# Input norm of an encoder trunk: two token tiles transposed through diag(1/rms), the gain moved to the split, and a written order on four engines

## The chip, the cores and the metric

The kernel runs on one core of a Trainium2 chip. The core has TensorE (PE, matrix products), VectorE (DVE), ScalarE (ACT), GpSimd (POOL) and SyncE (SP), which here only issues DMAs. Each engine works through its own queue in order. The metric is the device time of one execution in microseconds.

## The reference, cut to what matters

One layer of an encoder on 512 tokens of 1024 channels, in float32: a token mixer (HGRN2 and mLSTM heads behind one input projection), cross-attention to 256 memory tokens, an MLP with squared ReLU, and a final norm. The change touches only the first norm and the first use of what it gives:

```
def rmsnorm(x, g):
    y = x32 * lax.rsqrt(jnp.mean(x32 * x32, axis=-1, keepdims=True) + NORM_EPS)
    return (y * g.astype(jnp.float32)).astype(x.dtype)

proj = rmsnorm(x, norm_mix) @ w_in + b_in
```

`1/rms` belongs to a token, the gain `g` (`norm_mix`) to a channel. The columns of the projection that come first are 1536 to 2047, the value `h_i` of HGRN2 (512 columns), needed with the tokens on the partitions.

## The kernel before, in words

**Numbers.** A big product keeps float32 precision by splitting both operands into a rounded high half and a low half (`split_out`, lines 227 to 229: ACT copies the high half, DVE subtracts it from the source for the low half) and adding three products, high by high, high by low and low by high (`mm3`, lines 231 to 234). A split of a tile from PSUM reads it twice, once on each engine.

**The weights** come as a stream of blocks of 128 x 1024 floats (512 KB). `load(i)` (line 203) issues the DMA of block i on SP into one of three `st` buffers; `split(i)` (line 210) makes its halves `wh` and `wl`, three buffers each. `weights(key)` asks for the block, splits it and the two next, and loads the one after them.

**The first stage, lines 135 to 325.** x comes in four tiles of 128 tokens by 1024 channels, two in each of two `as` buffers (`xin`, `xtile`). Tile by tile: ACT squares the tile and sums along the row (line 297); DVE makes the mean square (line 172) and POOL takes its power of -1/2 (line 174, `rstd_of`); DVE multiplies each half of the tile with 1/rms, a number for each partition, and the gain, which stands in two PSUM banks of 512 columns that are the same on all partitions (`gmix`, line 144: products of a column of ones with the row of gains; line 302). PE turns the half over, four transposes of 128 x 128 against the identity (line 305), and `split_out` writes the halves into `xT`, where the channels are on the partitions. For channel block k, `xT[k // 4]` holds 512 columns of high half and 512 of low half, one for each token.

The projection of the 512 value columns (`proj_t`, line 258) takes four weight blocks q = 0 to 3, of two channel blocks each. A *part* (t, q) is the six products of token tile t with weight block q, summed in PSUM bank `acc[t]`. It runs q = 0, 1, 2 over all four t, then q = 3, where each t ends and is evacuated by DVE with a bias added (line 324). The bias is loaded in line 318 into a `T2` buffer of 516 columns, of which there are five. PSUM has four banks `mm` and four banks `sm`. The next stage is the product for the gates (lines 511 and 512), and behind it the other columns of the projection.

`small_setup` (line 146) loads the small vectors `vc` and the level masks, and makes some small constants on DVE and ACT. The identity is part of `cs`, 392 columns of constants loaded by ACT's queue (line 139).

**The order of the work.** The kernel is written with a tile framework: a planner puts the instructions of each engine in an order, by priority (`tc.high_priority`) and by when its plan finds their inputs ready, and inserts the waits. Only the MLP at the end has PE's order fixed as written (`tc.manual_schedule`, line 991).

Of the kernel before, what the change touches and what calls it, by code (L numbers as in the profile page):

```python
# [18 lines left out]
P = 128  # L19
S = 512  # L20
D = 1024
# [18 lines left out]
C_ID, C_MF, C_MB, C_SEL, NC1 = 0, 128, 256, 384, 392  # L40
# [39 lines left out]
def trunk(ctx: ExitStack, tc: tile.TileContext, x, mem, wpk, vec, cst, lmask, rmask, rows, out):  # L80
    nc = tc.nc
    big = ctx.enter_context(tc.tile_pool(name="big", bufs=1))
    sb = ctx.enter_context(tc.tile_pool(name="sb", bufs=1))
    psm = ctx.enter_context(tc.tile_pool(name="psm", bufs=4, space=PSUM))
    pss = ctx.enter_context(tc.tile_pool(name="pss", bufs=4, space=PSUM))
    v, sc, gp, pe = nc.vector, nc.scalar, nc.gpsimd, nc.tensor
    cnt = [0]

    def nm(s):
        cnt[0] += 1  # L90
        return f"{s}_{cnt[0]}"
# [28 lines left out]
    cs = sb.tile([P, NC1], F32, name="cs")  # L120
# [13 lines left out]
    def load_x(t):  # L134
        nc.sync.dma_start(out=xtile[t], in_=x[t * P:t * P + P, :])

    load_x(0)
    nc.scalar.dma_start(out=grow1[0:1, :], in_=rows[0:1, :])
    nc.scalar.dma_start(out=cs, in_=cst[:, 0:NC1])
    one1 = misc[0:1, 63:64]  # L140
    gp.memset(one1, 1.0)
    gmix = [mmb(), mmb()]
    for g in range(2):
        pe.matmul(gmix[g], lhsT=one1.to_broadcast([1, P]), rhs=grow1[0:1, g * 512:g * 512 + 512], start=True, stop=True)

    def small_setup():
        lmf = A4()
        nc.sync.dma_start(out=vc, in_=vec)
        nc.sync.dma_start(out=lmf[:, 0:len(LEVELS) * P], in_=lmask)
        for j in range(2):  # L150
            a = lmf[64 * j:64 * j + 64, 64 * j:NLV * P]
# [10 lines left out]
        v.tensor_copy(selr[0:64, :], cs[0:64, C_SEL:C_SEL + 8])  # L162
        v.tensor_copy(selr[64:128, :], cs[0:64, C_SEL:C_SEL + 8])
        v.tensor_scalar(out=negb, in0=vc[:, V_FF:V_FF + 8], scalar1=-1.0, scalar2=None, op0=ALU.mult)
# [5 lines left out]
    def rstd_of(ss, w, n):  # L170
        ms = tiny(w)
        v.tensor_scalar(out=ms, in0=ss, scalar1=1.0 / n, scalar2=EPS, op0=ALU.mult, op1=ALU.add)  # L172
        r = tiny(w)
        gp.tensor_tensor(out=r, in0=ms, in1=nh.to_broadcast([P, w]), op=ALU.pow)  # L174
        return r, ms
# [51 lines left out]
    def split_out(dst_hi, dst_lo, src):  # L227
        sc.activation(dst_hi, src, AF.Copy)  # L228
        v.tensor_tensor(out=dst_lo, in0=src, in1=dst_hi.bitcast(F32), op=ALU.subtract)  # L229

    def mm3(ps, ah, al, bh, bl, first, last):
        pe.matmul(ps, lhsT=ah, rhs=bh, start=first, stop=False)  # L232
        pe.matmul(ps, lhsT=ah, rhs=bl, start=False, stop=False)  # L233
        pe.matmul(ps, lhsT=al, rhs=bh, start=False, stop=last)  # L234
# [23 lines left out]
    def proj_t(mat, k0, c0, xs, ntile=4, pre=None, late=False):  # L258

        acc = [mmb() for _ in range(ntile)]  # L260

        def part(t, q, w):
            for k in range(2):
                kk = 2 * q + k
                xh, xl = xs[kk][0][:, t * P:t * P + P], xs[kk][1][:, t * P:t * P + P]
                z = slice(k * 512, k * 512 + 512)
                mm3(acc[t], xh, xl, w[0][:, z], w[1][:, z], kk == 0, kk == 7)

        for q in range(2 if late else 3):
            w = weights(("t", mat, k0 + 2 * q, c0))  # L270
            for t in range(ntile):
                part(t, q, w)
                if t % 2 == 1:
                    tick()
        if pre is not None:
            pre()
        tail = [(q, weights(("t", mat, k0 + 2 * q, c0))) for q in range(2 if late else 3, 4)]
        for t in range(ntile):
            for q, w in tail:
                part(t, q, w)  # L280
            yield t, acc[t]
            if t % 2 == 1:
                tick()


    xT = XT()
    load(0)
    load_x(1)
    load_x(2)
    load(1)  # L290
    load_x(3)

    junk = G4()
    for t in range(4):
        xt = xtile[t]
        ss = tiny(1)
        sc.activation(junk, xt, AF.Square, accum_out=ss)
        r, _ = rstd_of(ss, 1, D)
        with tc.high_priority():
            for g in range(2):  # L300
                xg = xt[:, g * 512:g * 512 + 512]
                v.scalar_tensor_tensor(out=xg, in0=xg, scalar=r, in1=gmix[g], op0=ALU.mult, op1=ALU.mult)
                ps = smb()
                for k in range(4):
                    pe.transpose(ps[:, k * P:k * P + P], xg[:, k * P:k * P + P], ident)
                p3 = ps[:, :].rearrange("p (k t) -> p k t", t=P)
                split_out(ap(xT[g], t * P, [1024, 4], [1, P]), ap(xT[g], 512 + t * P, [1024, 4], [1, P]), p3)
        if t < 2:
            split(t)
    small_setup()  # L310
    xs = xk(xT)


    vh = []

    def bias_row(i):
        b = T2()
        nc.sync.dma_start(out=b[:, 0:512], in_=rows[1 + i // 2:2 + i // 2, (i % 2) * 512:(i % 2) * 512 + 512].to_broadcast([P, 512]))
# [298 lines left out]
    def mv_proj():  # L617
        b = bias_row(1)
        for t, ps in proj_t("in", 0, 3584, xs):
            d = VV()  # L620
            gp.memset(ap(d, P, [129, 4], [1, 1]), 1.0)
            v.tensor_tensor(out=ap(d, 0, [129, 4], [1, P]), in0=ps[:, :].rearrange("p (h e) -> p h e", e=P),
                            in1=b[:, 0:512].rearrange("p (h e) -> p h e", e=P), op=ALU.add)
            mv.append(d)

    mq = {}
# [127 lines left out]
    for t in range(2):  # L754
        a = mt[t]
# [31 lines left out]
    for c in range(2):  # L787
        for t, ps in proj_t("kv", 0, 1024 + 512 * c, ms, 2):
            d = A4(F32R)
# [101 lines left out]
    for h in range(4):  # L891
        qd[h] = []
        for ps in proj_d("xq", 256 * h, x2):
            d = YT1()
# [97 lines left out]
    for f in range(4):  # L992
# [72 lines left out]
        while n < len(JOBS):  # L1065
            p, g = JOBS[n]
# [8 lines left out]
            w = ahead(n)  # L1075
# [95 lines left out]
```

## Time and profile before

| what | value |
|---|---|
| median of 3 runs (lowest to highest) | 861.6 us (861.53 to 861.63) |
| the profiled execution: its own time | 861.55 us |
| its span, first to last instruction | 859.8 us |
| PE busy in the span | 839.1 us (98%) |
| DVE, ACT, POOL busy | 566.8, 422.8, 67.4 us |
| granted PE clock, mean | 0.996 |
| time from HBM | 110.76 MB, 131 GB/s |

A row of a timeline has the start and the duration in us, the engine, the line, the operation, the tile written and the tiles read, their shape and how many instructions were merged; in brackets stands the idle time before it and what ended that. "L305" is line 305 of the kernel. Durations of PE overlap, as its instructions are pipelined, so the distance between starts says how fast it works. "PEld" is the load of the stationary operand, "SPq" and "ACTq" a DMA being issued on that engine's queue.

### The profile page before, as it was taken

The numbers are of one execution on the slowest core, as the hardware profiler recorded it, in microseconds if no ns is written. First come the engines' busy times: TensorE is split into PE (matmuls) and PEld (weight loads), VectorE is DVE, ScalarE is ACT, GpSimd is POOL, SyncE is SP. The second block draws the span as 40 slices with busy tenths as digits, with TensorE's granted clock in tenths as the row PEclk, the third lists the DMA queues.
The fourth block names the chain that finished last, engine by engine and source line by source line (L and its number), as shares of the span: only waits on it lengthen the run. The fifth ranks groups of instructions, "written<-read, shape, count | busy, mean of one in ns | idle before, by whom it ended". The sixth has DMA issues, their size and how long they took to land.

```text
span 859.8 us, 11677 instructions
## 1 busy us (share of the span) xinstructions
PE 839.1 (98%) x4438; PEld 692.3 (81%) x4438; DVE 566.8 (66%) x996; ACT 422.8 (49%) x773; POOL 67.4 (8%) x114
## 2 busy tenths in 40 slices
PE   7999999999999999999999999999999999999994
PEld 5888788788887987887888887888888888888883
DVE  5558874699437977654555446676667656756675
ACT  5336354445558576454443346453454344434544
POOL 1000000100100000100001200003101210220001
PEclk9999999999999999999999999999999999999998
DMA  6332224022252332542213852248935992697322
GB/s 265 126 117 78 70 77 139 31 74 88 80 141 74 99 125 98 177 117 98 74 50 117 201 147 82 95 132 234 277 112 142 276 243 98 177 290 193 123 50 98
DMA packets 32682, 113.62 MB, mean 132 GB/s; under 512 B 3761, under 2 KB 3889, under 8 KB 32626
## 3 DMA queue, kind: packets, MB, share of 16 engines
q1 hardware_dynamic: 23120, 78.84, 26.4%
q0 software_dynamic: 9216, 33.56, 17.7%
q8 instruction: 35, 0.57, 0.3%
q10 hardware_dynamic: 290, 0.47, 0.2%
q14 instruction: 21, 0.17, 0.1%
HBM read 110.76 MB, written 2.10 MB: 131 GB/s over the span
## 4 chain that ended last, share of the span: by engine, by line
PE 72%; issue 21%; DVE 3%; POOL 1%; DMA 1%; ACT 1%; POOLq 0%; ACTq 0%; DVEq 0%
PE mm L233 15%; PE mm L232 15%; PE mm L234 15%; PE sm L1045 5%; PE sm L1046 5%; PE sm L1047 5%; PE sm L682 2%; PE sm L667 2%; PE sm L380 1%; POOL tiny L174 1%; PE mm L1046 1%; PE mm L1045 1%; PE mm L1047 1%; PE sm L450 1%; DVE wl L229 1%
## 5 line engine op out<-in xcount | busy, mean ns | idle before, releaser
L228 ACT ACTIVATE wh<-st 128x1024 fp32r<-128x1024 f32 x133 | 141.0, 1060 | 222.7 <-PE mm L233 118.0
L229 DVE TENSOR_TENSOR wl<-st,wh 128x1024 fp32r<-128x1024 f32 x133 | 162.8, 1224 | 116.0 <-ACT wh L228 110.9
L232 PE MATMUL mm<-xT,wh 128*128 128x512 f32 x544 | 215.6, 397 | 0.0
L233 PE MATMUL mm<-xT,wh 128*128 128x512 f32 x544 | 213.2, 392 | 0.3 <-DVE xT L824 0.3
L234 PE MATMUL mm<-xT,wl 128*128 128x512 f32 x544 | 212.5, 391 | 0.0
L233 PEld LDWEIGHTS mm<-xT,wh 128*128 128x128 f32 x544 | 102.2, 188 | 22.9 <-DVE xT L824 2.0
L232 PEld LDWEIGHTS mm<-xT,wh 128*128 128x128 f32 x544 | 102.2, 188 | 22.2 <-issue 0.7
L234 PEld LDWEIGHTS mm<-xT,wl 128*128 128x128 f32 x544 | 102.1, 188 | 21.4 <-issue 0.2
L939 POOL DMA_DIRECT2D as<-in_wpk x48 | 36.5, 771 | 312.5 <-DVE wl L229 186.7
L1003 DVE SCALAR_TENSOR_TENSOR t<-mm,rg 128x512 f32<-128x512 f32 x32 | 22.1, 691 | 55.1 <-PE mm L234 55.0
L234 PE MATMUL mm<-wh,yT 128*128 128x512 f32 x128 | 50.6, 395 | 0.0
L232 PE MATMUL mm<-wh,yT 128*128 128x512 f32 x128 | 50.4, 394 | 0.0
L233 PE MATMUL mm<-wl,yT 128*128 128x512 f32 x128 | 50.0, 391 | 0.0
L1045 PE MATMUL sm<-wh,yT 128*128 128x512 f32 x128 | 49.8, 389 | 0.0
L1046 PE MATMUL sm<-wl,yT 128*128 128x512 f32 x128 | 49.8, 389 | 0.0
L1047 PE MATMUL sm<-wh,yT 128*128 128x512 f32 x128 | 49.8, 389 | 0.0
L228 ACT ACTIVATE wh<-as 128x1024 fp32r<-128x1024 f32 x24 | 25.5, 1062 | 33.3 <-PE sm L1047 23.7
L229 DVE TENSOR_TENSOR wl<-as,wh 128x1024 fp32r<-128x1024 f32 x24 | 29.4, 1225 | 13.9 <-ACT wh L228 13.9
L174 POOL TENSOR_TENSOR tiny<-tiny,misc 128x1 f32<-128x1 f32 (+1 forms) x18 | 14.2, 788 | 299.0 <-DVE tiny L172 299.0
L978 DVE TENSOR_TENSOR vv<-vv,sm 128x512 f32<-128x512 f32 x48 | 31.0, 680 | 1.2 <-PE sm L1047 1.2
L228 ACT ACTIVATE yT<-t 128x512 fp32r<-128x512 f32 x32 | 19.8, 629 | 17.0 <-DVE t L1020 16.5
L1045 PEld LDWEIGHTS sm<-wh,yT 128*128 128x128 f32 x128 | 24.0, 188 | 5.0
(273 smaller groups left out, 1503.4 us busy)
## 6 DMA issues: line engine op xcount, KB each, us to landing
st<-in_wpk SPq DMA_DIRECT2D x133, 512.0 KB, 3.4
as<-in_wpk POOLq DMA_DIRECT2D x48, 512.0 KB, 6.6
gate<-in_wpk POOLq DMA_DIRECT2D x16, 512.0 KB, 7.0
as<-in_x SPq DMA_DIRECT2D x4, 512.0 KB, 6.5
vv<-in_x SPq DMA_DIRECT2D x8, 256.0 KB, 3.6
out<-vv SPq DMA_DIRECT2D x7, 256.0 KB, 2.3
a<-in_mem SPq DMA_DIRECT2D x2, 512.0 KB, 5.8
t<-in_rows SPq DMA_DIRECT2D x2, 256.0 KB, 6.1
```

The source lines that it names most:

```text
L174: gp.tensor_tensor(out=r, in0=ms, in1=nh.to_broadcast([P, w]), op=ALU.pow)
L228: sc.activation(dst_hi, src, AF.Copy)
L229: v.tensor_tensor(out=dst_lo, in0=src, in1=dst_hi.bitcast(F32), op=ALU.subtract)
L232: pe.matmul(ps, lhsT=ah, rhs=bh, start=first, stop=False)
L233: pe.matmul(ps, lhsT=ah, rhs=bl, start=False, stop=False)
L234: pe.matmul(ps, lhsT=al, rhs=bh, start=False, stop=last)
L939: gp.dma_start(out=dst, in_=wpk[idx], **kw)
L978: v.tensor_tensor(out=z, in0=z, in1=ps, op=ALU.add if sign > 0 else ALU.subtract)
L1003: v.scalar_tensor_tensor(out=y, in0=ps, scalar=0.0, in1=rrow[:, 0:512], op0=ALU.max, op1=ALU.mult)
L1045: pe.matmul(ps, lhsT=ah, rhs=bh, start=new, stop=False, **fl)
L1046: pe.matmul(ps, lhsT=ah, rhs=bl, start=False, stop=False, **fl)
L1047: pe.matmul(ps, lhsT=al, rhs=bh, start=False, stop=end and k == 1, **fl)
```

## The change

1. **Gain.** The two banks of broadcast gains go. Eight products of one column each put the gain on the partitions, channel block by channel block, in `gk` (128 x 8), which ACT copies out of PSUM. The gain is multiplied in when the turned tile is split (`x_split`): ACT's copy takes it as its scale, and DVE's instruction becomes a `scalar_tensor_tensor`.
2. **Tiles 0 and 1** are not scaled. DVE makes diag(1/rms) from the identity (`x_diag`), and the turn is an ordinary float32 product of the tile with that matrix (`x_turn`), which scales as it transposes. **Tiles 2 and 3** are scaled by DVE with 1/rms alone (`x_scale`) and transposed as before.
3. **Halves.** A split takes 256 columns: one channel block of two token tiles (0 and 1, then 2 and 3). A PSUM bank holds two channel blocks of a token half, so that four banks hold a half.
4. **Order.** From the first square to part (1, 2) the order on PE, DVE, ACT and POOL is the order in which the code is written (`tc.manual_schedule`). The other parts follow in `proj_vh`.
5. **Loads.** ACT's queue loads the identity alone; the other constants follow on SP inside `small_setup`. Block 1 is loaded ahead of tile 2, and block 2 behind tile 3.
6. **Setup and bias** go behind the split of the second half. The masks are loaded into the buffer of tiles 0 and 1, the bias into that of tile 2.

```diff
-    nc.scalar.dma_start(out=cs, in_=cst[:, 0:NC1])
+    nc.scalar.dma_start(out=ident, in_=cst[:, C_ID:C_ID + P])
...
-    gmix = [mmb(), mmb()]
-    for g in range(2):
-        pe.matmul(gmix[g], lhsT=one1.to_broadcast([1, P]), rhs=grow1[0:1, g * 512:g * 512 + 512], start=True, stop=True)
+    gk = sb.tile([P, 8], F32, name="gk")
+    pg = smb()
+    for k in range(8):
+        pe.matmul(pg[:, k:k + 1], lhsT=grow1[0:1, k * P:k * P + P], rhs=one1, start=True, stop=True)
+    sc.activation(gk, pg[:, 0:8], AF.Copy)
 
     def small_setup():
-        lmf = A4()
+        lmf = xin[0]
         nc.sync.dma_start(out=vc, in_=vec)
+        nc.sync.dma_start(out=cs[:, P:NC1], in_=cst[:, P:NC1])
...
     load(0)
     load_x(1)
+    load(1)
     load_x(2)
-    load(1)
     load_x(3)
+    load(2)
...
-    for t in range(4):
-        xt = xtile[t]
-        ss = tiny(1)
-        sc.activation(junk, xt, AF.Square, accum_out=ss)
-        r, _ = rstd_of(ss, 1, D)
-        with tc.high_priority():
-            for g in range(2):
-                xg = xt[:, g * 512:g * 512 + 512]
-                v.scalar_tensor_tensor(out=xg, in0=xg, scalar=r, in1=gmix[g], op0=ALU.mult, op1=ALU.mult)
-                ps = smb()
-                for k in range(4):
-                    pe.transpose(ps[:, k * P:k * P + P], xg[:, k * P:k * P + P], ident)
-                p3 = ps[:, :].rearrange("p (k t) -> p k t", t=P)
-                split_out(ap(xT[g], t * P, [1024, 4], [1, P]), ap(xT[g], 512 + t * P, [1024, 4], [1, P]), p3)
-        if t < 2:
-            split(t)
-    small_setup()
+    def x_stat(t):
+        ss = tiny(1)
+        sc.activation(junk, xtile[t], AF.Square, accum_out=ss)
+        rx[t], _ = rstd_of(ss, 1, D)
+
+    def x_diag(t):
+        v.tensor_scalar(out=dg[:, t * P:t * P + P], in0=ident, scalar1=rx[t], scalar2=None, op0=ALU.mult)
+
+    def x_scale(t):
+        for g in range(2):
+            z = xtile[t][:, g * 512:g * 512 + 512]
+            v.tensor_scalar(out=z, in0=z, scalar1=rx[t], scalar2=None, op0=ALU.mult)
+
+    def x_turn(t, g):
+        for k in range(4 * g, 4 * g + 4):
+            if (t // 2, k // 2) not in xbank:
+                xbank[t // 2, k // 2] = smb()
+            o = (k % 2) * 256 + (t % 2) * P
+            ps = xbank[t // 2, k // 2][:, o:o + P]
+            a = xtile[t][:, k * P:k * P + P]
+            if t < 2:
+                pe.matmul(ps, lhsT=a, rhs=dg[:, t * P:t * P + P], start=True, stop=True)
+            else:
+                pe.transpose(ps, a, ident)
+
+    def x_split(u, ks):
+        for k in ks:
+            ps = xbank[u, k // 2][:, (k % 2) * 256:(k % 2) * 256 + 256]
+            o = (k % 4) * 1024 + u * 256
+            hi, lo = xT[k // 4][:, o:o + 256], xT[k // 4][:, o + 512:o + 768]
+            g = gk[:, k:k + 1]
+            last_x[:] = [sc.activation(hi, ps, AF.Copy, scale=g),
+                         v.scalar_tensor_tensor(out=lo, in0=ps, scalar=g, in1=hi.bitcast(F32), op0=ALU.mult, op1=ALU.subtract)]
+
+    acc_v = [mmb() for _ in range(4)]
+
+    def part_v(t, q):
+        w = hl_tiles[q]
+        for k in range(2):
+            kk = 2 * q + k
+            z = slice(k * 512, k * 512 + 512)
+            mm3(acc_v[t], xs[kk][0][:, t * P:t * P + P], xs[kk][1][:, t * P:t * P + P], w[0][:, z], w[1][:, z], kk == 0, kk == 7)
+
+    with tc.high_priority(), tc.manual_schedule(engines={ET.PE, ET.DVE, ET.Activation, ET.Pool}):
+        x_stat(0)
+        x_diag(0)
+        x_stat(1)
+        x_turn(0, 0)
+        x_diag(1)
+        x_turn(1, 0)
+        split(0)
+        x_split(0, range(4))
+        split(1)
+        part_v(0, 0)
+        x_turn(0, 1)
+        part_v(1, 0)
+        x_turn(1, 1)
+        x_split(0, range(4, 8))
+        part_v(0, 1)
+        part_v(1, 1)
+        x_stat(2)
+        x_stat(3)
+        x_scale(2)
+        split(2)
+        x_scale(3)
+        for g in range(2):
+            x_turn(2, g)
+            x_turn(3, g)
+            x_split(1, range(4 * g, 4 * g + 4))
+            part_v(g, 2)
...
-    bvh = bias_row(0)
-    for t, ps in proj_t("in", 0, 1536, xs):
+    def proj_vh():
+        for q in range(3):
+            part_v(2, q)
+            part_v(3, q)
+            with tc.high_priority():
+                split(q + 3)
+        load(6)
+        for t in range(4):
+            part_v(t, 3)
+            yield t, acc_v[t]
+
+    pv = proj_vh()
+    bvh = xin[1][:, 0:512]
+    for t, ps in pv:
+        if t == 0:
+            bias_row(0, bvh)
+            with tc.issue_after(last_x[0].ins), tc.issue_after(last_x[1].ins):
+                small_setup()
         d = VV()
-        v.tensor_tensor(out=d[:, 0:512], in0=ps, in1=bvh[:, 0:512], op=ALU.add)
+        v.tensor_tensor(out=d[:, 0:512], in0=ps, in1=bvh, op=ALU.add)
         vh.append(d)
```

More of the change, by code (lines that the diff above doesn't have):

```diff
@@ L288, in trunk @@
     load_x(1)
+    load(1)
     load_x(2)
-    load(1)
     load_x(3)
+    load(2)
+    xs = xk(xT)
     junk = G4()
-    for t in range(4):
-        xt = xtile[t]
+    rx, dg, xbank = {}, T2(), {}
+    def x_stat(t):
         ss = tiny(1)
-        sc.activation(junk, xt, AF.Square, accum_out=ss)
-        r, _ = rstd_of(ss, 1, D)
-        with tc.high_priority():
-            for g in range(2):
-                xg = xt[:, g * 512:g * 512 + 512]
-                v.scalar_tensor_tensor(out=xg, in0=xg, scalar=r, in1=gmix[g], op0=ALU.mult, op1=ALU.mult)
-                ps = smb()
-                for k in range(4):
-                    pe.transpose(ps[:, k * P:k * P + P], xg[:, k * P:k * P + P], ident)
-                p3 = ps[:, :].rearrange("p (k t) -> p k t", t=P)
-                split_out(ap(xT[g], t * P, [1024, 4], [1, P]), ap(xT[g], 512 + t * P, [1024, 4], [1, P]), p3)
-        if t < 2:
-            split(t)
@@ L310, in trunk @@
-    small_setup()
-    xs = xk(xT)
+        sc.activation(junk, xtile[t], AF.Square, accum_out=ss)
[17 more added lines that the diff above has]
+                pe.transpose(ps, a, ident)
@@ new lines, in x_split @@
+    def x_split(u, ks):
[6 more added lines that the diff above has]
+                         v.scalar_tensor_tensor(out=lo, in0=ps, scalar=g, in1=hi.bitcast(F32), op0=ALU.mult, op1=ALU.subtract)]
+    last_x = []
+    acc_v = [mmb() for _ in range(4)]
@@ new lines, in part_v @@
+    def part_v(t, q):
[4 more added lines that the diff above has]
+            mm3(acc_v[t], xs[kk][0][:, t * P:t * P + P], xs[kk][1][:, t * P:t * P + P], w[0][:, z], w[1][:, z], kk == 0, kk == 7)
+    ET = mybir.EngineType
+    with tc.high_priority(), tc.manual_schedule(engines={ET.PE, ET.DVE, ET.Activation, ET.Pool}):
[25 more added lines that the diff above has]
+            part_v(g, 2)
@@ L314, in trunk, with bias_row @@
     vh = []
-    def bias_row(i):
-        b = T2()
-        nc.sync.dma_start(out=b[:, 0:512], in_=rows[1 + i // 2:2 + i // 2, (i % 2) * 512:(i % 2) * 512 + 512].to_broadcast([P, 512]))
-        return b
-    bvh = bias_row(0)
-    for t, ps in proj_t("in", 0, 1536, xs):
+    def bias_row(i, b=None):
+        b = b or T2()[:, 0:512]
+        nc.sync.dma_start(out=b, in_=rows[1 + i // 2:2 + i // 2, (i % 2) * 512:(i % 2) * 512 + 512].to_broadcast([P, 512]))
+        return b
+    def proj_vh():
[8 more added lines that the diff above has]
+            yield t, acc_v[t]
@@ L622, in mv_proj @@
             v.tensor_tensor(out=ap(d, 0, [129, 4], [1, P]), in0=ps[:, :].rearrange("p (h e) -> p h e", e=P),
-                            in1=b[:, 0:512].rearrange("p (h e) -> p h e", e=P), op=ALU.add)
+                            in1=b.rearrange("p (h e) -> p h e", e=P), op=ALU.add)
             mv.append(d)
```

## The prediction

> **What bounds the kernel now.** I read the page first (busy shares, then the chain), after it the busy time by stage, and last the first 40 us in order of time. The page, for the whole program:
>
> ```profile
> span 859.8 us, 11677 instructions
> PE 839.1 (98%) x4438; PEld 692.3 (81%) x4438; DVE 566.8 (66%) x996; ACT 422.8 (49%) x773; POOL 67.4 (8%) x114
> PE 72%; issue 21%; DVE 3%; POOL 1%; DMA 1%; ACT 1%; POOLq 0%; ACTq 0%; DVEq 0%
> ```
>
> TensorE (PE) sets the end. A step elsewhere is worth what it moves PE's start, its gaps or its own work. By stage (us, then PE busy, PEld, DVE, ACT, POOL):
>
> ```profile
> 0.00:20.00 20.00, 14.32 (x53) 10.12 (x54) 10.58 (x21) 11.85 (x19) 2.95 (x16) 1.00 0.75 285
> 20.00:40.00 20.00, 19.82 (x92) 16.20 (x91) 13.13 (x22) 6.09 (x8) 1.33 (x3) 1.00 0.30 106
> 40.00:80.00 40.00, 39.91 (x186) 32.66 (x185) 27.45 (x67) 20.09 (x26) 0.00 (x0) 1.00 0.32 104
> 80.00:200.00 120.00, 118.55 (x904) 97.60 (x903) 91.54 (x148) 56.69 (x99) 2.57 (x10) 1.00 0.25 82
> 200.00:300.00 100.00, 99.27 (x632) 83.10 (x631) 69.13 (x136) 60.95 (x139) 5.87 (x14) 1.00 0.30 95
> ```
>
> After 20 us PE hardly ever stops: what the first product of the next stage (the gates, line 511) gains or loses, the end gains or loses too. The stage changed is the one before it; PE's timeline (start, duration):
>
> ```profile
> 9.43 1.97 PE L305 MATMUL sm<-cs,as 128*128 128x128 f32 x8 [3.42 <-DVE as L302]
> 11.23 0.79 PE L232 MATMUL mm<-wh,xT 128*128 128x512 f32 x1
> 11.82 0.63 PE L233 MATMUL mm<-wl,xT 128*128 128x512 f32 x1
> 12.25 1.05 PE L305 MATMUL sm<-cs,as 128*128 128x128 f32 x4
> ...
> 13.95 0.41 PE L233 MATMUL mm<-wl,xT 128*128 128x512 f32 x1
> ...
> 14.43 0.60 PE L305 MATMUL sm<-cs,as 128*128 128x128 f32 x4
> 14.78 0.48 PE L232 MATMUL mm<-wh,xT 128*128 128x512 f32 x1
> ...
> 22.09 0.40 PE L234 MATMUL mm<-wh,xT 128*128 128x512 f32 x1
> ...
> 37.51 0.39 PE L511 MATMUL mm<-xT,wh 128*128 128x512 f32 x1
> ```
>
> Starts tell more than durations, which overlap. From 22.09 to 37.51 stand 68 products: 15.42 / 68 = 0.227 us each, so one part (six products of a token tile with one weight block) takes 1.36. Four transposes take 0.35 (14.43 to 14.78). Until about 14 us PE is slow: 0.43 for one product (11.82 to 12.25), 1.97 for eight transposes. The next stage starts at 37.51; that number the change has to beat. What the stage needs at full speed is 16 parts and 32 transposes, 21.8 + 2.8 = 24.6 us from 9.43, or 34.0: only 3.5 us are lost now, 2.3 or so of them to the slow clock.
>
> **What starts the stage.** The other engines, and the transfers (KB, us from issue to landing):
>
> ```profile
> 4.47 1.06 ACT L297 ACTIVATE gate<-as 128x1024 f32<-128x1024 f32 x1 [1.67 <-DMA as<-in_x]
> 5.65 0.15 DVE L172 TENSOR_SCALAR tiny<-tiny 128x1 f32<-128x1 f32 x1 [5.65 <-ACT gate L297]
> 5.88 0.56 POOL L174 TENSOR_TENSOR tiny<-tiny,misc 128x1 f32<-128x1 f32 x1 [4.91 <-DVE tiny L172]
> 7.11 0.16 DVE L162 CAST selr<-cs 64x8 fp32r<-64x8 f32 x1 [1.31 <-DMA cs<-in_cst]
> 8.63 1.40 DVE L302 SCALAR_TENSOR_TENSOR as<-as,tiny,mm 128x512 f32<-128x512 f32 x2
> 11.07 1.05 ACT L297 ACTIVATE gate<-as 128x1024 f32<-128x1024 f32 x1
> 12.11 0.59 ACT L228 ACTIVATE xT<-sm 128x512 fp32r<-128x512 f32 x1
> 1.65 0.97 SPq L135 DMA_DIRECT2D as<-in_x  x2
> as<-in_x SPq DMA_DIRECT2D x1, 512.0 KB, 6.1
> cs<-in_cst ACTq DMA_DIRECT2D x1, 196.0 KB, 5.7
> ```
>
> Tile 0's 1/rms is ready at 6.44, 1.97 after its square began, but DVE scales the tile only at 8.63: it had queued a cast that waits for the constants (7.11). Tile 1 is issued at 1.65 and lands at 7.75. A square holds ACT for 1.04 (11.07 to 12.11).
>
> **The change, part by part.** Removed are eight scalings on DVE (L302), 16 of the 32 transposes, and the two 512-column gain broadcasts. Added are gk, two diagonals, 16 fp32 products for tiles 0 and 1, four plain scalings, 16 pairs of splits at 256 columns. Rows of the same forms elsewhere in this trace:
>
> ```profile
> 147.45 7.31 PE L450 MATMUL sm<-vv,as 128*128 128x128 f32 x64
> 249.96 1.56 ACT L776 ACTIVATE a<-sm,vc 128x256 fp32r<-128x256 f32 x4
> 250.66 3.36 DVE L777 SCALAR_TENSOR_TENSOR a<-sm,vc,a 128x256 fp32r<-128x256 f32 x8
> L353 DVE TENSOR_SCALAR a<-a,misc 128x512 f32<-128x512 f32 x8 | 3.8, 481 | 0.0
> L507 DVE CAST wh<-wl 128x128 fp32r<-128x128 f32 x1 | 0.2, 228 | 0.1
> L229 DVE TENSOR_TENSOR wl<-st,wh 128x1024 fp32r<-128x1024 f32 x8 | 9.8, 1225 | 8.3 <-ACT wh L228 8.2
> L228 ACT ACTIVATE wh<-st 128x1024 fp32r<-128x1024 f32 x8 | 8.5, 1057 | 13.7 <-PE mm L234 10.6 <-PE mm L512 2.6 <-DMA st<-in_wpk 0.5
> L550 PE MATMUL sm<-tiny,a 128*128 128x32 f32 x10 | 1.2, 267 | 0.0
> 1.36 0.36 ACTq L139 DMA_DIRECT2D cs<-in_cst  x1
> ```
>
> *Products with the diagonal.* L450 issues two instructions for one fp32 product; 7.31 / 64 = 0.114 each, so 0.23 a product against 0.09 a transpose. A turn of four costs 0.91, slow clock 1.83. The 16 of them add 16 x 0.14 = 2.2 us of PE work; turn (0,0) lies in PE's wait for tile 1.
>
> *Start.* Part 0 now needs both tiles of the half, since a split covers 256 columns of bank and order. Tile 1 lands earlier, because 196 KB of constants become 64: tile 1 at 7.75 and 512 KB per 1.3 us give 0.3 for the 132 KB, so 7.4. (The identity alone, issued at 1.36, lands at 7.06 at the latest, the old landing of cs; turn (0,0) may begin as late as 7.9 without holding up tile 1.) Square at 7.4, 1/rms at 9.4, diagonal (0.23 by L507, taken as 0.3) 9.7, turn (1,0) from 9.75. So PE's path starts no sooner than the 9.43 of now: the stall on the constants moves to the landing of tile 1. ACT also does tile 1's square before block 0's split, which waits till 8.5 instead of 6.11; hidden, block 0 is split by 10.9.
>
> *First parts.* Slow turn (1,0) to 11.55; its first bank done 10.7, split pairs at 0.36 on ACT and 0.41 on DVE keep pace. I take full speed from about 12: part (0,0) ends 13.15, turn (0,1) 14.05, part (1,0) 15.4, first bank of turn (1,1) at X = 15.9, its end 16.3, parts (0,1) and (1,1) to 19.05. Until here nothing waits.
>
> *Tiles 2 and 3.* Here the written order decides. ACT's queue holds four splits, Sq2, Sq3, block 2's split, and the four splits wait for turn (1,1), which PE does behind part (1,0). ACT has been idle since about 13.2 (splits of channels 0 to 3 from 10.7, then block 1's, 1.06), with tile 2 landed near 10 and tile 3 near 11.5 (the old landings are 9 and 11.6), and cannot begin. After X: four splits 1.5, Sq2 from X + 1.5, Sq3 from X + 2.55, block 2's high half X + 3.6 to 4.65. DVE's queue: the mean square of tile 3 at X + 3.7, *ahead of* tile 2's scaling, which so waits for tile 3 too: X + 3.9 to 4.75 (0.42 a half; L353 overlaps). Then block 2's low half to X + 5.95, and only behind it tile 3's scaling, first half at X + 6.4. PE: turn (2,0) at 20.3, idle 1.25; turn (3,0) at 22.3, idle 1.65. Parts (0,2) and (1,2) could fill 2.7 us but stand behind these turns.
>
> *Rest.* 12 parts and 12 transposes: 16.3 + 1.1 = 17.4, so the next stage starts at 39.7: 2.2 us later than 37.51. Full speed from turn (1,0) on would give 38.75 (+1.25; the low half of block 0, ready at 10.9, then holds the first part), slow clock until 14 us 40.6 (+3.1). The eight gk products are 16 instructions of one column. L550's 0.12 each, doubled for the slow clock, is 3.9 from 2.26, done at 6.2 in PE's wait; at nothing each they change nothing either. If gk's copy stands ahead of tile 0's square on ACT, that square slips to 6.4 and turn (1,0) by 0.9 (upper bound).
>
> *Moved setup.* SP's order changes to x0, w0, x1, w1, x2, x3, w2; the masks, vec, the other constants and the bias go behind the later weights, into the two x buffers. Block 6 waits for block 3's split, near 31.5; the bias issues near 32 and, with the 3.4 to 8 us that transfers take here, lands by 40, and the first bank is needed again at 39.7, its evacuation 0.7 before. I price that at 0, at most 1. The small DVE casts come from 7.11 to a stage where DVE is a third idle: 0.
>
> **Sum.** The profiled execution took 861.55 (span 859.8 and 1.75 around it), the median is 861.6, so they may be used alike. 861.6 + 2.2 = 863.8; the likeliest case's own range 862.8 to 865.2.
>
> [...]
>
> **Rivals.**
> (a) The clock falls in the gaps. For: after 3.42 us of idle PE ran slow from 9.43 to 13.95. Against: the gaps here are shorter and interrupted. Price: 4.5 us at half speed, 2.2: 866.0.
> (b) Not slower: the order is not kept as written on ACT and DVE, so that tile 2's and 3's squares run when they land (10 to 12.5) and PE never waits in the middle. Then from 9.75: 1.83, 0.5 of slow clock, 16 parts 21.8, two turns 1.8, 16 transposes 1.4: 37.1, or 36.0 at full speed. That is 860.1 to 861.6, say 861.2. It decides where tile 3 is turned before 19.4. For: squares ran early in the profile of now (11.07). Against: the diff names ACT and DVE in its fixed order.
> (c) The part after 40 us is planned anew, with one 516-column buffer that the bias no longer holds. PE's idle in 80 to 300 us is 1.45 + 0.73 = 2.2; losing all of it gives 861.6 with my start and 859.0 with (b)'s, which I take to be this case's usual company. The same planning can cost as much. Nothing in the profile says which.
>
> **How the numbers follow.** About 0.2%, 1.7 us, is what can be told from no change: 859.9 to 863.3. My case 55%, a quarter of it below 863.3; (a) 10%; (b) 22%; (c) 13%, faster in two thirds. Slower 0.41 + 0.10 = 0.51; same 0.14 + 0.20 + 0.04 = 0.38; faster 0.02 + 0.09 = 0.11. The range leaves out (c)'s faster part, the lower end of (b) and the upper half of (a): 860.4 to 866.0.
>
> **What will show it.** Right: turn (1,0) near 9.75; ACT idle before the splits of channels 4 to 7; ACT's square of tile 2 after 17; PE idle some 3 us between 19 and 22.5; line 511's counterpart near 39.7; PE busy up by 2.2. Wrong: tile 2's square before 14, or that counterpart before 38; slow products after the gaps speak for (a); a stage that starts late with a span that doesn't, for (c).

## The result, and the profile after

The changed kernel takes 870.16 us in the median, against 861.53 us (861.00 to 861.63) for the kernel before: ratio 1.0102, interval 1.009 to 1.0115. Four executions lie between 869.63 and 870.43 us; a fifth, of 4692.88 us, stays out of the ratio. Forecast were 863.8 us and a range up to 866.0. The sign was right, and the size was four times too small.

The page of the kernel after has the span and the busy times:

```profile
span 868.7 us, 11749 instructions
PE 845.0 (97%) x4466; PEld 699.3 (81%) x4466; DVE 565.8 (65%) x1002; ACT 425.2 (49%) x782; POOL 67.4 (8%) x114
```

PE still sets the end. The busy time by stage of the kernel after (us, then PE, PEld, DVE, ACT, POOL, the granted PE clock, the DMA share, GB/s) says where it lost:

```profile
0.00:20.00 20.00, 15.88 (x68) 14.34 (x69) 5.93 (x12) 8.95 (x16) 1.55 (x9) 1.00 0.75 272
20.00:40.00 20.00, 15.78 (x69) 12.29 (x68) 10.74 (x21) 9.12 (x16) 2.74 (x9) 0.91 0.34 104
```

Between 20 and 40 us PE is busy for 15.78 us where it was busy for 19.82, and the granted clock is 0.91 where it was 1.00. For 0 to 20 us it reads 1.00 in both kernels although the first products are slow, because the record of the clock in these traces begins only when full speed is reached (at 13.96 before, at 16.11 after). Until then "the slow clock" is read from the distance between products alone: 0.43 us, and 0.227 at full speed. PE's timeline of the kernel after (L325 is the product with the diagonal, L327 a transpose, L235 to L237 the three products of `mm3`, L592 and L593 the gates):

```profile
9.74 2.08 PE L325 MATMUL sm<-t,as 128*128 128x128 f32 x8 [0.71 <-DVE t L309]
11.59 0.80 PE L235 MATMUL mm<-wh,xT 128*128 128x512 f32 x1
...
14.31 1.91 PE L325 MATMUL sm<-t,as 128*128 128x128 f32 x8
...
16.30 0.39 PE L236 MATMUL mm<-wl,xT 128*128 128x512 f32 x1
...
17.46 1.05 PE L325 MATMUL sm<-t,as 128*128 128x128 f32 x8
...
20.86 0.39 PE L237 MATMUL mm<-wh,xT 128*128 128x512 f32 x1
23.93 0.63 PE L327 MATMUL sm<-cs,as 128*128 128x128 f32 x4 [2.69 <-issue]
26.09 0.91 PE L327 MATMUL sm<-cs,as 128*128 128x128 f32 x4 [1.53 <-DVE as L314]
...
27.23 0.63 PE L236 MATMUL mm<-wl,xT 128*128 128x512 f32 x1
27.66 0.63 PE L235 MATMUL mm<-wh,xT 128*128 128x512 f32 x1
...
30.71 0.39 PE L235 MATMUL mm<-wh,xT 128*128 128x512 f32 x1
...
49.14 0.39 PE L237 MATMUL mm<-wh,xT 128*128 128x512 f32 x1
50.20 0.50 PE L235 MATMUL mm<-xT,wh 128*128 128x512 f32 x1 [0.68 <-ACT a L595]
```

The planner put unwritten work, later parts and the gates, between the written instructions, so that the gates no longer lie behind the last part. The row to compare is the stage behind the gates, 50.20 here. In PE's timeline of the kernel before it is

```profile
41.14 0.39 PE L232 MATMUL mm<-xT,wh 128*128 128x512 f32 x1
```

That is 9.06 us later, and from there to the end of the span both kernels need the same: 868.7 - 50.20 = 818.5 and 859.8 - 41.14 = 818.7. All of the loss lies before this point. By starts (a product at full speed is 0.227, four diagonal products 0.81 by 17.46 to 18.27, four transposes 0.35):

| where | after | before | difference |
|---|---|---|---|
| first turn that PE waits for (turn (1,0); tile 0 before) | 9.74 | 9.43 | +0.31 |
| work from there at full speed: 16 parts 21.8, gates 3.6, and 12 diagonal products and 16 transposes (before: 32 transposes) | 29.26 | 28.23 | +1.03 |
| lost to the slow clock until it opens (16.30; 13.95) | 3.35 | 2.56 | +0.79 |
| PE's gaps, 21.09 to 23.93 and 24.28 to 26.09 | 4.65 | 0 | +4.65 |
| lost to the slow clock behind the gaps, 26.09 to 30.71 | 1.78 | 0 | +1.78 |
| wait for the evacuation of the gates, 49.37 to 50.20 | 0.83 | 0 | +0.83 |
| rest | 0.59 | 0.92 | -0.33 |

The gaps come out of ACT's and DVE's queues. Their timelines in the kernel after (L335 and L336 are the two halves of `x_split`, L305 the square, L175 the mean square, L314 the scaling of tiles 2 and 3, L231 and L232 the two halves of a weight split, L595 the evacuation of the gates):

```profile
18.10 0.47 ACT L335 ACTIVATE xT<-sm,gk 128x256 fp32r<-128x256 f32 x1 [3.18 <-PE sm L325]
19.12 0.84 ACT L335 ACTIVATE xT<-sm,gk 128x256 fp32r<-128x256 f32 x2 [0.55 <-DVE xT L336]
20.54 0.47 ACT L335 ACTIVATE xT<-sm,gk 128x256 fp32r<-128x256 f32 x1 [0.58 <-DVE xT L336]
20.91 1.05 ACT L305 ACTIVATE gate<-as 128x1024 f32<-128x1024 f32 x1
...
22.08 1.06 ACT L305 ACTIVATE gate<-as 128x1024 f32<-128x1024 f32 x1
...
47.57 2.01 ACT L231 ACTIVATE wh<-st 128x1024 fp32r<-128x1024 f32 x2 [5.80 <-PE mm L593]
49.48 0.67 ACT L595 ACTIVATE a<-mm,vc 128x512 f32<-128x512 f32 x1
```

```profile
18.61 0.48 DVE L336 SCALAR_TENSOR_TENSOR xT<-sm,gk,xT 128x256 fp32r<-128x256 f32 x1 [2.43 <-ACT xT L335]
...
23.26 0.15 DVE L175 TENSOR_SCALAR tiny<-tiny 128x1 f32<-128x1 f32 x1 [1.03 <-ACT gate L305]
23.35 0.88 DVE L314 TENSOR_SCALAR as<-as,tiny 128x512 f32<-128x512 f32 x2
24.21 1.22 DVE L232 TENSOR_TENSOR wl<-st,wh 128x1024 fp32r<-128x1024 f32 x1
25.36 1.07 DVE L314 TENSOR_SCALAR as<-as,tiny 128x512 f32<-128x512 f32 x2
```

ACT is idle for 3.18 us, then takes four splits, and only then squares tiles 2 and 3, whose data had long landed. The scaling of tile 2 stands behind tile 3's mean square (23.26), that of tile 3 behind the low half of a weight block. The prediction had this chain. What it lacked is the 0.55 us between ACT's first and second split and the 0.58 before the fourth: two channel blocks lie in one PSUM bank, and ACT's read of the second begins only when DVE's of the first is over. Of the third, which is in another bank, it does not wait. So four splits take 2.81 us (18.10 to 20.91), not 1.5. The wait ahead of 50.20 comes from ACT too: it does two weight splits (47.57) before it evacuates the gates (49.48).

### The profile page after: what moved, and what is told of

Read it like the earlier page. It is cut to its first block, busy times and chain, and to the rows that moved or that the text cites. A ratio compares the mean times of both kernels' runs of the same rounds, so it can differ in the third digit from the quotient of the medians.

```text
span 868.7 us, 11749 instructions
## 1 busy us (share of the span) xinstructions
PE 845.0 (97%) x4466; PEld 699.3 (81%) x4466; DVE 565.8 (65%) x1002; ACT 425.2 (49%) x782; POOL 67.4 (8%) x114
## 4 chain that ended last, share of the span: by engine, by line
PE 72%; issue 21%; DVE 2%; ACT 1%; POOL 1%; DMA 1%; SPq 0%; POOLq 0%; ACTq 0%; DVEq 0%
PE mm L235 15%; PE mm L237 15%; PE mm L236 15%; PE sm L1126 5%; PE sm L1128 5%; PE sm L1127 5%; PE sm L763 2%; PE sm L748 2%; PE sm L461 1%; POOL tiny L177 1%; PE mm L1126 1%; PE mm L1128 1%; PE mm L1127 1%; PE sm L531 1%; DMA as<-in_x 1%
## 5 line engine op out<-in xcount | busy, mean ns | idle before, releaser
L231 ACT ACTIVATE wh<-st 128x1024 fp32r<-128x1024 f32 x133 | 140.9, 1060 | 218.7 <-PE mm L236 117.8
L232 DVE TENSOR_TENSOR wl<-st,wh 128x1024 fp32r<-128x1024 f32 x133 | 162.6, 1223 | 118.5 <-ACT wh L231 113.4
L235 PE MATMUL mm<-xT,wh 128*128 128x512 f32 x544 | 215.7, 397 | 0.7 <-ACT a L595 0.7
L237 PE MATMUL mm<-xT,wl 128*128 128x512 f32 x544 | 212.4, 391 | 0.0
L235 PEld LDWEIGHTS mm<-xT,wh 128*128 128x128 f32 x544 | 102.2, 188 | 23.1 <-ACT a L595 1.1
L237 PEld LDWEIGHTS mm<-xT,wl 128*128 128x128 f32 x544 | 102.1, 188 | 21.5 <-issue 0.2
L237 PE MATMUL mm<-wh,yT 128*128 128x512 f32 x128 | 50.6, 395 | 0.0
L235 PE MATMUL mm<-wh,yT 128*128 128x512 f32 x128 | 50.5, 394 | 0.0
L231 ACT ACTIVATE wh<-as 128x1024 fp32r<-128x1024 f32 x24 | 25.5, 1062 | 33.3 <-PE sm L1128 23.7
L232 DVE TENSOR_TENSOR wl<-as,wh 128x1024 fp32r<-128x1024 f32 x24 | 29.4, 1225 | 13.9 <-ACT wh L231 13.9
L1127 PEld LDWEIGHTS sm<-wl,yT 128*128 128x128 f32 x128 | 24.0, 188 | 5.0
```

The costliest lines, as they stand in the source:

```text
L1127: pe.matmul(ps, lhsT=ah, rhs=bl, start=False, stop=False, **fl)
```

## Experiments

All are compared with the kernel before, measured beside them: its median there was 861.44 us for e1 to e4, 861.32 for e5 to e8 and 861.28 for e9. "Next stage" is the start of the stage behind the gates in the profiled execution; the span less that start is between 818.3 and 818.7 us in every row.

| kernel | median, us | ratio, interval | span | next stage |
|---|---|---|---|---|
| after | 870.16 | 1.0102 (1.009 to 1.0115) | 868.7 | 50.20 |
| e1_early | 867.05 | 1.0071 (1.0054 to 1.0088) | 864.4 | 45.97 |
| e2_fill | 867.69 | 1.0074 (1.0059 to 1.0089) | 866.5 | 48.10 |
| e3_transp | 868.06 | 1.0078 (1.0063 to 1.0093) | 865.8 | 47.46 |
| e4_alt | 868.50 | 1.0079 (1.0064 to 1.0094) | 866.8 | 48.35 |
| e5_loads | 860.91 | 0.9996 (0.9988 to 1.0005) | 859.5 | 40.88 |
| e6_first | 861.91 | 1.0008 (0.9998 to 1.0017) | 860.9 | 42.29 |
| e7_warm | 870.65 | 1.0108 (1.0094 to 1.0121) | 869.0 | 50.64 |
| e8_sum | 862.99 | 1.0019 (1.001 to 1.0028) | 861.0 | 42.73 |
| e9_splits | 860.26 | 0.9987 (0.9978 to 0.9996) | 858.8 | 40.24 |

### The squares and scalings of tiles 2 and 3 written earlier

```diff
         part_v(0, 0)
+        x_stat(2)
+        x_stat(3)
+        x_scale(2)
+        x_scale(3)
...
         part_v(1, 1)
-        x_stat(2)
-        x_stat(3)
-        x_scale(2)
         split(2)
-        x_scale(3)
```

> The squares and the scalings of tiles 2 and 3 are written ahead of the second half's splits (behind block 1's split), block 2's split behind part (1, 1); nothing else differs from the changed kernel. Theory (the written order on ACT and DVE makes PE wait, and the wait lets its clock fall): the waits before the turns (2, 0) and (3, 0), 2.84 and 1.80 us, go, the products behind them start 0.23 apart instead of 0.43, and 870.2 falls by 4.6 + 1.7 to about 863.9. Rival 1 (the fp32 products with the diagonal are the cost, PE waits for them anyway): the waits only move, time within 1 us of 870.2. Rival 2 (the stages after 40 us, planned anew, are the cost): within 1 us of 870.2 as well, although the waits go.

It took 867.05 us (866.12 to 868.23). PE's timeline, and ACT's and DVE's, in this kernel:

```profile
21.07 1.03 PE L327 MATMUL sm<-cs,as 128*128 128x128 f32 x8
23.63 0.86 PE L235 MATMUL mm<-wh,xT 128*128 128x512 f32 x2 [1.53 <-ACT wh L231]
24.33 0.39 PE L236 MATMUL mm<-wl,xT 128*128 128x512 f32 x1
```

```profile
18.06 0.47 ACT L335 ACTIVATE xT<-sm,gk 128x256 fp32r<-128x256 f32 x1 [0.95 <-PE sm L325]
20.74 0.84 ACT L335 ACTIVATE xT<-sm,gk 128x256 fp32r<-128x256 f32 x2 [2.21 <-DVE xT L336]
```

```profile
17.23 3.09 DVE L314 TENSOR_SCALAR as<-as,tiny 128x512 f32<-128x512 f32 x4
```

Both turns run at 21.07 without a wait, so the written place of the squares and scalings is what made PE's two gaps. But the gain is 3.1 us where 6.3 were expected, because DVE's four scalings (3.09 us) now hold up its first split of the second half, ACT waits 2.21 us for the shared bank, and block 2 of the weights is split late: a new gap of 23.63 - 21.77 = 1.86 us. Behind that one gap PE stays at full speed: the two products from 23.63 take 0.70 with the restart, and the granted clock between 20 and 40 us is 1.00. The wait for block 2 was not foreseen.

### The gaps filled with products that are thrown away

```diff
+    def fill(n):
+        for _ in range(n):
+            pe.matmul(acc_v[3], lhsT=xs[0][0][:, 0:P], rhs=hl_tiles[0][0][:, 0:512], start=True, stop=True)
...
         for g in range(2):
+            if g == 0:
+                fill(11)
             x_turn(2, g)
+            if g == 0:
+                fill(7)
             x_turn(3, g)
```

> 18 products whose result is thrown away (a bank that is cleared later) stand in PE's two waits, 11 before turn (2, 0) and 7 before turn (3, 0), 0.227 us each at full speed. PE's work grows, its stream doesn't start earlier. Theory (the waits let the clock fall): transposes and products behind turn (3, 0) at full speed from the start, 1.7 us gained, 868.5. Rival (the slow products from 26 to 29.6 us have another cause, as the waits for weights or splits): nothing gained, 870.2 or above.

867.69 us (867.12 to 868.24). PE's timeline:

```profile
21.13 2.65 PE L350 MATMUL mm<-wh,xT 128*128 128x512 f32 x11
23.98 0.63 PE L327 MATMUL sm<-cs,as 128*128 128x128 f32 x4 [0.19 <-issue]
24.36 1.86 PE L350 MATMUL mm<-wh,xT 128*128 128x512 f32 x7
26.15 0.66 PE L327 MATMUL sm<-cs,as 128*128 128x128 f32 x4
26.56 0.47 PE L235 MATMUL mm<-wh,xT 128*128 128x512 f32 x1
26.87 0.40 PE L236 MATMUL mm<-wl,xT 128*128 128x512 f32 x1
```

The real turns start where they did, 23.98 and 26.15, but the first products behind them start 0.31 apart (26.56, 26.87) where they were 0.57 apart (26.66, 27.23), and the granted clock between 20 and 40 us is 1.00 again. So the products behind the gaps had been slow because the clock had fallen behind the gaps of 2.84 and 1.81 us. The kernel with the useless work is 2.5 us faster, but not all of that is the clock. In the profiled execution the next stage starts 2.1 us earlier: 1.3 of that is the clock (from 26.15 to 29.43, 11 products and four transposes lose 0.44, where it was 1.78), and 0.8 is the wait for the evacuation of the gates, which this kernel does not show.

### No diagonal: all four tiles scaled and transposed

```diff
-        v.tensor_scalar(out=dg[:, t * P:t * P + P], in0=ident, scalar1=rx[t], scalar2=None, op0=ALU.mult)
+        x_scale(t)
...
-            if t < 2:
-                pe.matmul(ps, lhsT=a, rhs=dg[:, t * P:t * P + P], start=True, stop=True)
-            else:
-                pe.transpose(ps, a, ident)
+            pe.transpose(ps, a, ident)
```

> Tiles 0 and 1 are scaled by DVE like tiles 2 and 3 and turned by transposes; no diagonal. Theory: 16 fp32 products of 0.23 us become transposes of 0.09; turns (0, 1) and (1, 1) give X, the end of the last turn's first bank, about 1.5 to 2 us earlier, and all that waits for X with it; about 868.2. The waits in the middle stay near 4.6 us. Rival 1 (the fp32 products are the cost of the change): near 863, most of the 8.6 gone.

868.06 us (867.37 to 868.71). PE's gaps are still there:

```profile
22.11 0.63 PE L324 MATMUL sm<-cs,as 128*128 128x128 f32 x4 [2.91 <-issue]
24.27 1.12 PE L324 MATMUL sm<-cs,as 128*128 128x128 f32 x4 [1.53 <-DVE as L314]
```

So the float32 products are not the main cost. Everything up to 22.11 comes 1.82 us earlier than in the changed kernel, which is about what the prediction put down for them (2.2); but the clock also opened earlier in this execution (transposes at full speed from 14.03, products in the changed kernel from 16.30), so the two are not separated. The next stage starts 2.74 us earlier; 0.83 of that is the wait for the evacuation of the gates, which this kernel does not show either.

### The splits taken from the two banks in turn

```diff
     def x_split(u, ks):
-        for k in ks:
+        for k in [ks[i] for i in (0, 2, 1, 3)]:
```

> The four channel blocks of a split go in the order 0, 2, 1, 3, so that consecutive ones lie in different PSUM banks. In the changed kernel ACT starts a second block of a bank only when DVE has read the first (0.55 us of idle, twice in four). Theory: that wait goes, four splits take about 1.7 instead of 2.8 us, X and turn (3, 0) come 1.1 to 1.3 us earlier, 869.0; the first part may start later by up to 0.5, as it needs blocks 0 and 1. If the wait is not the bank's but the engines' order: no change, 870.2.

868.50 us (866.74 to 868.62). ACT's splits and PE's turns:

```profile
17.22 1.95 ACT L335 ACTIVATE xT<-sm,gk 128x256 fp32r<-128x256 f32 x4 [2.90 <-PE sm L325]
19.07 1.05 ACT L305 ACTIVATE gate<-as 128x1024 f32<-128x1024 f32 x1
```

```profile
22.09 0.63 PE L327 MATMUL sm<-cs,as 128*128 128x128 f32 x4 [1.73 <-issue]
24.25 0.94 PE L327 MATMUL sm<-cs,as 128*128 128x128 f32 x4 [1.53 <-DVE as L314]
```

Four splits without a wait take 1.85 us, not 2.81: the shared bank is worth 0.96 us on the chain. The next stage starts 1.85 us earlier; the other 0.89 is the clock, which in this execution opened at about 14.3. The clock fell again, to 0.91 between 20 and 40 us.

### The loads and the setup alone

The kernel before, with the identity alone on ACT's queue and `small_setup` behind the last split of x.

```diff
-    nc.scalar.dma_start(out=cs, in_=cst[:, 0:NC1])
+    nc.scalar.dma_start(out=ident, in_=cst[:, C_ID:C_ID + P])
...
-    small_setup()
...
+        if t == 0:
+            with tc.issue_after(last_x[0].ins), tc.issue_after(last_x[1].ins):
+                small_setup()
```

> The kernel before with the moved loads and the moved setup of the change alone: ACT's queue loads the identity only (64 instead of 196 KB), the other constants come on SP inside the setup, and the setup stands behind the last split of x. Theory: DVE no longer waits for the constants until 7.11 us; its next instruction is the low half of weight block 0 (about 7.0 to 8.2), so tile 0 is scaled some 0.5 us earlier, 861.4 becomes about 860.9, within 0.2%; this part of the change costs nothing. Rival (the moved setup is part of the 8.6 us lost): 1 us or more above 861.4.

860.91 us (860.48 to 861.29), against 861.32: no difference. PE's first transposes:

```profile
8.74 1.97 PE L305 MATMUL sm<-cs,as 128*128 128x128 f32 x8 [2.72 <-DVE as L302]
```

They start 0.69 us earlier than the 9.43 of before, and the next stage 0.26 earlier. The moved constants and setup cost nothing (the order of the weight loads was left as before), and an earlier start is largely lost to the slow clock, which lasted to about 14.8 here (four transposes from 14.12 to 14.81, 0.69 where 0.35 is full speed).

### Before's work in a written order, tile 0's scalings first

On the kernel before, the loads and setup of the change, and a fixed order on DVE, ACT and POOL only.

```diff
+    with tc.high_priority(), tc.manual_schedule(engines={ET.DVE, ET.Activation, ET.Pool}):
+        x_stat(0)
+        x_scale(0, 0)
+        x_scale(0, 1)
+        split(0)
...
+        x_scale(1, 1)
+        x_stat(2)
+        x_out(1, 0)
+        split(1)
+        x_out(1, 1)
+        x_scale(2, 0)
+        x_stat(3)
+        x_scale(2, 1)
+        x_out(2, 0)
+        split(2)
```

> As before in its work (gain and 1/rms multiplied by DVE, transposes, splits of 512 columns), with the moved loads and setup, the loads in the order of the change, and an order written for DVE, ACT and POOL: tile 0's two scalings first, then block 0's split, then tile by tile; PE's order is the planner's. Theory (work goes as early as its inputs are there, and nothing ready stands behind something that isn't): first product near 9.4 instead of 11.23 us, no long waits, 1 to 2 us gained on 861.4: 859.4 to 860.4. Rival (an order written out costs as such, or the slow clock at the start eats what an earlier start brings): 861.4 or above.

861.91 us (861.44 to 862.90), no gain. The first product runs at 9.16 (11.23 before), and PE then waits (its timeline):

```profile
13.63 0.50 PE L232 MATMUL mm<-wh,xT 128*128 128x512 f32 x1 [0.69 <-ACT xT L229]
...
20.11 0.73 PE L232 MATMUL mm<-wh,xT 128*128 128x512 f32 x2 [0.64 <-ACT wh L229]
21.37 0.50 PE L233 MATMUL mm<-wl,xT 128*128 128x512 f32 x1 [0.53 <-DVE wl L229]
```

The last two rows have the same fault as the change: a weight split written behind work that waits for PE.

### PE warmed by products that are thrown away

```diff
+    def fill(n):
+        pe.matmul(acc_v[3][:, 0:n], lhsT=xtile[0][:, 0:P], rhs=xtile[0][:, 0:n], start=True, stop=True)
...
+        fill(256)
         x_turn(0, 0)
+        fill(192)
```

> The changed kernel with two fp32 products of 256 and 192 columns, thrown away, in PE's waits before turn (0, 0) and turn (1, 0), so that PE works without a break of more than 0.5 us from 2.4 us on. Theory (the clock opens some time after PE began to work without a break): full speed some 2 to 4 us earlier than at 14 to 16.3 us, X and all behind it 1 to 2 us earlier, 868 to 869. Rival (when the clock opens isn't set by those short waits): no earlier, 870.2.

870.65 us (869.75 to 870.95). PE's timeline:

```profile
4.47 1.22 PE L349 MATMUL mm<-as 128*128 128x256 f32 x2 [4.47 <-DMA as<-in_x]
5.62 3.57 PE L145 MATMUL sm<-misc,rg 1*128 1x1 f32 x16
9.12 2.08 PE L325 MATMUL sm<-t,as 128*128 128x128 f32 x8
...
14.88 0.40 PE L235 MATMUL mm<-wh,xT 128*128 128x512 f32 x1
```

The fill pushed the gain's products, and so the first turns, back by 2 us; so this does not tell what warming would be worth. It shows that PE, hardly idle from 4.47 on, was still slow at 14.1 and fast at 14.88. What opens the clock stays open.

### The causes taken away together

All four tiles transposed, banks in turn, the squares and scalings of tiles 2 and 3 and the weight splits earlier, parts up to q = 2 inside the written order.

```diff
+        x_stat(2)
+        x_stat(3)
+        x_scale(2)
...
+        x_scale(3)
-        for g in range(2):
-            x_turn(2, g)
...
+        x_split(1, range(4))
+        part_v(0, 2)
+        part_v(1, 2)
+        x_turn(2, 1)
```

> The causes taken together: all four tiles scaled by DVE and transposed, channel blocks split in the order 0, 2, 1, 3, squares and scalings of tiles 2 and 3 written ahead of the second half's splits, tile 3's scaling behind them, block 2's split ahead of tile 2's turns, and parts up to q = 2 of all tiles inside the written order. Theory: no wait over 0.5 us between the first part and the end of the stage, the clock stays up, 870.2 - 4.6 - 1.7 - 2.2 = 861.7 or a little below. Rival (something else in the change costs: halves of two tiles, gain at the split, the moved loads): 864 or above although PE doesn't wait in the middle.

862.99 us (862.44 to 863.86), against 861.32: the loss is 1.7 us where it was 8.6, with halves, the gain at the split and a written order kept and the diagonal gone. One of its remaining waits, in PE's timeline:

```profile
21.33 0.50 PE L236 MATMUL mm<-wl,xT 128*128 128x512 f32 x1 [0.35 <-DVE wl L232]
```

The granted clock between 20 and 40 us is 1.00. The kernel is still slower than before, its interval above 1. The time lies between the forecast of 861.7 and the 864 of the rival, and what the last 1.7 us are is not shown.

### The weight splits written where they are needed

The order of e6, with blocks 1 and 2 split earlier, and each tile's square and scalings moved by a step.

```diff
         split(0)
-        x_stat(1)
         x_out(0, 0)
-        x_scale(1, 0)
+        x_stat(1)
         x_out(0, 1)
+        x_scale(1, 0)
         x_scale(1, 1)
-        x_stat(2)
-        x_out(1, 0)
         split(1)
+        x_out(1, 0)
+        x_stat(2)
         x_out(1, 1)
+        split(2)
         x_scale(2, 0)
-        x_stat(3)
         x_scale(2, 1)
+        x_stat(3)
         x_out(2, 0)
-        split(2)
-        x_scale(3, 0)
         x_out(2, 1)
+        x_scale(3, 0)
```

> Edit: the kernel of the written order with tile 0's scalings first (e6), with the splits of weight blocks 1 and 2 and the third square moved ahead in that order: split(1) directly behind the scalings of tile 1, split(2) behind the four splits of tiles 0 and 1. In e6 the first product ran at 9.16 us, but TensorE then waited 0.69 us before 13.63 (for ScalarE's split of tile 1, and the half block behind it), 0.64 before 20.11 and 0.53 before 21.37 (both for weight block 2), and its stage after the gates started at 42.29. Theory (these waits are all that e6 lost against the kernel before, and they come from the order in which blocks 1 and 2 were written): the two waits for block 2 go, 1.2 us, that before 13.63 stays at least in part, since ScalarE cannot split tile 1 before its transposes; the stage after the gates starts at about 41.1, time 860.7, and at best 860.2. Rival (the clock opens at its own time, so what TensorE does earlier it does at half speed): the waits go, but full speed comes later than in e6 (13.5 us) and the time stays at 861.9. A second rival (a written order moves its waits elsewhere): new waits of the same size, 861.9 or more.

860.26 us (859.92 to 860.68), against 861.28: 1.0 us faster than the kernel before, the interval just under 1. PE's timeline:

```profile
13.78 0.51 PE L232 MATMUL mm<-wh,xT 128*128 128x512 f32 x1 [0.25 <-ACT xT L229]
...
40.24 0.39 PE L232 MATMUL mm<-xT,wh 128*128 128x512 f32 x1
```

Both waits for block 2 are gone, 0.25 us is left before 13.78, and the next stage starts at 40.24, 0.9 us earlier than the 41.14 of before. So the loss of e6 lay in its written order. That the two waits, 1.2 us, came from where block 2 was split is read from the traces, as squares and scalings moved in this edit too. This version, the work of the kernel before in another order, beats the kernel before by little and the changed kernel by 9.9 us (860.26 against 870.16).

## Why the prediction was right, and where it was wrong

**Right.** PE sets the end and the stages behind the gates shift as a block (818.5 and 818.7 us); the rival of a new plan there falls. Turn (1,0) starts at 9.74, forecast 9.75. The order is kept as written on ACT and DVE, so the rival "not slower" falls. PE waits twice, ahead of turns (2,0) and (3,0), and the second wait is 1.81 us for 1.65 forecast. e1 shows that the written place of the squares and scalings makes these gaps, e5 that the moved constants and setup cost nothing.

**Wrong: the size.** Forecast was +2.2; measured is +9.1 at the next stage of the profiled executions, +8.6 in the medians. The terms that account for it:

1. *"I take full speed from about 12."* It came at 16.30. The slow clock cost 3.35 us where the steps of the prediction have 1.1 (a slow turn, 0.9, and half of 11.55 to 12): 2.2 us too little. The bound "until 14" was the time of the kernel before, taken as if it were a constant. Part of this is chance: e4, with the same order on PE up to there, was fast from about 14.3 and began the second half's splits 0.88 us earlier.
2. *"Four splits 1.5."* They take 2.81, 1.3 more. The cadence came from rows (lines 776 and 777) in which each block has a bank of its own; the change packs two blocks into a bank. Squares follow at 1.17, not 1.05. Gap 1 became 2.84 instead of 1.25, both gaps 4.65 instead of 2.9: 1.75. e4 confirms the bank with 0.96 us on one set of four splits.
3. *Rival (a)* was given 10% as another way; it came on top. It cost 1.78 us (2.2 forecast), and e2 shows it: with the same gaps filled, the clock stays up. The argument against it, that these gaps are shorter than the 3.42 us ahead of the slow start and interrupted, does not hold: gaps of 2.84 and 1.81 us, with 0.35 us of transposes between them, were enough (as were 1.88 and 1.81 in e4). But PE had no product at all from 21.09 to 26.66, 5.57 us, only transposes. In e1 PE was without a product from 21.07 to 23.63, 2.56 us, and the clock stayed up. Whether the gaps or the time without a product counts, no run here tests by itself.
4. *"12 parts and 12 transposes: 17.4"* supposed that nothing waits behind the gaps. The planner drew the gates forward, and the first product of the next stage waits 0.83 us for their evacuation. That a written order binds only the instructions inside it, and that others are put in between, was in no step.

2.2 + 1.75 + 1.8 + 0.8 make 6.6 of the 6.9 us that were missing; 0.3 is spread. The diagonal products were forecast to add 2.2 us of work. At full speed one takes 0.20 us (0.81 for four) and a transpose 0.09, so that the 12 on the way cost 1.4; e3, which has none, did not separate them from the clock.

**When the clock changes.** The record of the granted clock has half speed from 26.35 to 29.76 here, 3.41 us. It begins with the opening at 16.11, 10.24 us ahead of the fall, which is three times 3.41. From 29.76 on full speed lasts 832.85 us, and in the kernel before 839.68 us from its opening at 13.96: 244 and 246 times 3.413, each until some 4.8 us behind PE's last product. So every stretch between two changes in these two traces is a multiple of 3.41 us. The openings lie 2.73 us (before) and 4.52 us (after) behind the first products (11.23, 11.59), so in these two traces the clock does not open at a fixed time behind the first product. In e4 and e3 the granted clock between 20 and 40 us is 0.91, which makes about 3.6 us of half speed (0.09 x 20 / 0.5), and in e7 0.83, about 6.8: an estimate from means of two digits. In all four traces with a fall PE starts only transposes for some time ahead of the slow products: between the starts 20.86 and 26.66 here, 19.98 and 24.84 in e4, 18.81 and 25.03 in e3, 21.25 and 27.27 in e7.

**Open.** What makes the clock open. It is not the amount of work alone: e7 worked PE from 4.47 and was slow until after 14.1, e4 ran the order of the changed kernel up to there and was fast at 14.3, where that one was slow until 16.1. Profiles of several executions of one kernel would be needed. Whether the transposes between the gaps bear on the fall is open too.

## What to carry to other kernels

An order written by hand is read engine by engine: for each entry that waits for PE, ask what stands behind it that could have run already, weight splits above all; moving a few such lines was worth 3.1 us from the changed kernel to e1 and 1.7 from e6 to e9. Gaps of PE can cost more than their length: two, of 2.84 and 1.81 us with only transposes between them, cost the clock as well, 1.78 us. And a cadence taken from another place of the trace holds only if the buffers are laid out the same way: here two engines reading one PSUM bank took turns, at 0.55 us for each second block.

## What the runs showed that was not expected

- The granted clock falls behind two gaps of 2.84 and 1.81 us, and 18 useless products in them make the kernel 2.5 us faster (867.69 against 870.16), more than half of it by the clock.
- Each stretch of the granted clock between two changes, in the traces of the kernels before and after, is a multiple of 3.41 us (246 of it before; 3, 1 and 244 after); half speed lasted 3.41 us in the changed kernel and about 6.8, by estimate, in e7.
- The time at which PE reaches full speed is 13.95 us in one kernel and 16.30 in another, whose first products differ by less than half a microsecond (11.23 and 11.59), and an earlier start of 0.69 us (e5) brings 0.26.
- A split of two channel blocks in one bank costs 0.55 us of wait for each second block, because ACT and DVE read it in turn; other banks in between hide it (e4).
